# Two encoder layers in one kernel: attention scores contracted over 128 rows, norm weights spread by matmuls, and a new order at four places

## The chip, the cores and the metric

The kernel runs on one core of a Trainium2 chip, in one launch. The metric is the device time of an execution in microseconds (us); smaller is better. Engines by the names of the profile: PE (TensorE) multiplies, PEld is its loading of stationary operands, DVE (VectorE) and ACT (ScalarE) do elementwise work, POOL (GpSimd) does little here, SP (SyncE) issues the DMAs. The profile also gives the share of its full clock that TensorE was granted.

## The reference

Two layers act on x, 256 rows of 1024. Each layer is a mixer of four branches and a gated convolutional FFN; a last norm follows.

```python
for layer in range(DEPTH):                                # 2
    u = rms_norm(x, norm_mix_g[layer])
    proj = einsum('bsd,de->bse', u, w_in[layer])          # 1024 -> 8976
    (a_in, bq, bk, bv, cq, ck, cv, co, cgate, dq, dk, dv, gates) = split_cols(proj)
    y_a = fourier_mix(a_in)
    y_b = gqa_branch(bq, bk, bv, qk_norm_g[layer], cos, sin)      # 8 q heads, 2 kv heads of 64
    y_c = mlstm_branch(cq, ck, cv, co, cgate, ...)                # 4 heads of 128, both directions
    y_d = diff_branch(dq, dk, dv, ..., rel_bias, layer + 1)       # 4 heads, 2 maps of 64 each
    branch = einsum('bsnc,ncd->bsnd', stack([y_a, y_b, y_c, y_d], 2), w_branch[layer])
    merged = sum(sigmoid(gates) * branch, axis=2)
    x = x + merged @ w_out[layer]
    v = rms_norm(x, norm_ffn_g[layer])
    x = x + conv_ffn(v, w_up[layer], conv_w[layer], conv_b[layer], w_down[layer])
return rms_norm(x, final_norm_g)
```

All of it is float32. The kernel keeps near that precision by splitting an operand into a rounded part and its residual.

## The kernel before, in words

**Split operands.** `weights` (from line 158) loads a tile of weights into one of four `raw` buffers by a DMA on SP, casts it on ACT to a rounded `hi` (L167) and forms the residual `lo` on DVE (L168); `raw` is free when both are done. Their slots come from tags: `whi` and `wlo` with three each (called STD), `ys` and `L` with six and five (ALT), or single buffers borrowed from work that is over. `mm3` then runs three matmuls: hi by hi, hi by lo, lo by hi. Activations are split alike: `transposed` puts four 128x128 transposes on PE into one PSUM buffer, and `split_T` makes hi on ACT (L244, or L247 with a scale) and lo on DVE (L245, L248).

**Row tiles.** The 256 rows are two row tiles, t = 0 and 1. `normed` adds the incoming sum to x where there is one (L267), squares both halves of 512 columns on ACT (L268), finds the reciprocal root on DVE by a series of one-column operations (L201 to L206) and scales by it and by the norm's weights (L270, L273, L275, L277). `normed_T` returns a function, `place`, that puts the transposes of its result into PE's order. The norm's weights come through `gain`, a DMA that broadcasts one row of 1024 to 128 partitions (L300).

**First projections.** `first_blocks` takes, for each row tile, `place`, then k, v and mLSTM's gate columns (272 columns, L371 onwards) and then the q columns of GQA, all eight blocks of the contraction.

**The order of the work.** PE's order is the program's order: `Flow` pins each matmul and transpose behind the one before. It also runs a planned clock of PE time (matmul columns at full speed) and holds the four branches as generators; at each `tick` a branch whose wait in `LATENCY`, counted on that clock, is over puts its next step into the order. So the branches' steps lie between the weight projections. On ACT, DVE and SP the Tile scheduler orders instructions by a simulation of its own; program order sets their priority, `tc.high_priority` raises it, and `tc.issue_after(ins)` puts what a block contains behind `ins` on that engine. Slots of a tag are handed out to tiles that ask for them. ACT and DVE execute their instructions in the resulting order.

**Score calls.** In GQA's and the differential branch's `scores`, q is stacked: `stacked` writes hi of a head of 64 into one half of the 128 partitions and its residual into the other (L323, L324). The keys' hi stands in both halves, so one matmul over 128 rows yields (q_hi + q_lo) k_hi. A second matmul over 64 rows adds q_hi k_lo. One call runs eight of them; a layer has four calls in each branch. In the differential branch the two maps have stacked keys `dk[0]` and `dk[1]` (tags `L`, `bk`) and share `dk[2]` (tag `dx`), which holds each map's residual in its own half; the function `keys` fills them (L1063 to L1065).

**The out projection.** `out_proj` goes through w_out in four steps of 256 rows (`kh` 0, 2, 4, 6) by two halves of 512 columns. The first step's tiles are used for both row tiles at once. Then the second half of merged is transposed (`mT[1]`, two tiles of tag `L`; `mT[0]` has two more), then come the tiles of the other steps: STD and ALT for `kh` 2, STD for 4, and (`gate`, `mg0`), (`gate`, `mg1`) for 6. Row tile 0 is finished first, and the ffn norm runs on it while row tile 1 is multiplied.

**The FFN.** `ffn` computes the first pair of column blocks (`first_pair`) for each row tile as its norm gets ready, later pairs for all 256 rows. `up_tiles(1)`, the second pair's weights, stands behind two recorded instructions, `ends[nc.scalar]` and `ends[nc.vector]`, through `issue_after`. `down` adds the second matmul, and the next layer's norm begins as the last of it ends.

Of the kernel before, what the change touches and what calls it, by code (L numbers as in the profile page):

```python
# [10 lines left out]
F32 = mybir.dt.float32  # L11
# [8 lines left out]
P = 128  # L20
S = 256
# [9 lines left out]
NEG = -1.0e30  # L31
URGENT = 1000
MIDS = 7
LATENCY = {
    "gqa": (10.0, 3.0, 4.5, 3.2, 2.0, 1.5),
    "fourier": (2.5,),
    "mlstm": (1.7, 12.1, 3.6, 0.6, 4.6, 1.0, 2.0, 9.9, 0.8, 7.6, 5.6, 6.0, 8.0),
    "diff": (1.6, 6.0, 4.5, 2.6, 7.8),
}
EARLY = 2  # L40
# [80 lines left out]
def body(nc, tc, A, out, const, work, psum, dram):  # L121
# [119 lines left out]

    def split_T(src_ps, hi, lo, scale=None):
        if scale is None:
            nc.scalar.copy(hi, src_ps)  # L244
            nc.vector.tensor_sub(lo, src_ps, hi)  # L245
        else:
            nc.scalar.activation(hi, src_ps, AF.Copy, scale=scale)  # L247
            nc.vector.scalar_tensor_tensor(lo, src_ps, scale, hi, ALU.mult, ALU.subtract)  # L248

    def transposed(src, t, hi, lo, scale=None, at=0):  # L250
        ps = scr()
        for j in range(4):
            tr(ps[:, j * P : (j + 1) * P], src[:, j * P : (j + 1) * P], ident)
        c = slice(t * P, (t + 1) * P)
        split_T(four(ps), hi[:, at : at + 4, c], lo[:, at : at + 4, c], scale)

    ends = {}

    def normed(t, g, emit, add=None):
        with tc.high_priority(offset=URGENT):  # L260
            ss = small(2, tag="ss")
            cs = slice(0, 512), slice(512, 1024)
            xs = [x_sb[t][:, c] for c in cs]
            ys = [mid() for _ in cs]
            for half in range(2):
                if add is not None:
                    nc.vector.tensor_add(xs[half], xs[half], add[half])  # L267
                nc.scalar.activation(mid(), xs[half], AF.Square, scale=2.0 ** 13 / math.sqrt(D), accum_out=ss[:, half : half + 1])  # L268
            if add is not None:
                nc.vector.tensor_mul(ys[0], xs[0], g[:, cs[0]])  # L270
            r = rsqrt_of_two(ss)
            if add is None:
                nc.vector.scalar_tensor_tensor(ys[0], xs[0], r, g[:, cs[0]], ALU.mult, ALU.mult)  # L273
            else:
                ends[nc.scalar] = nc.scalar.activation(ys[0], ys[0], AF.Copy, scale=r)  # L275
            emit(0, ys[0])
            ends[nc.vector] = nc.vector.scalar_tensor_tensor(ys[1], xs[1], r, g[:, cs[1]], ALU.mult, ALU.mult)  # L277
            emit(1, ys[1])

    def normed_T(t, g, pair, add=None):  # L280

        halves = []
        normed(t, g, lambda half, xn: halves.append(xn), add)

        def place():
            with tc.high_priority(offset=URGENT):
                for half in range(2):
                    transposed(halves[half], t, *pair, at=4 * half)

        return place  # L290

# [6 lines left out]
    def gain(src, tag, cols, eng=None):  # L298
        g = work.tile([P, cols], F32, tag=tag, name=nm(tag))
        (eng or nc.sync).dma_start(g, src.partition_broadcast(P))  # L300
        return g

    def win(layer, c0, width):
# [59 lines left out]
    def first_blocks(uT, sets, qsets, places):  # L363
        hi, lo = uT
        kv, q = [acc() for _ in range(NT)], [acc() for _ in range(NT)]
        for t in range(NT):
# [9 lines left out]
            for k in range(KD):  # L376
                wh, wl = qsets[k // 2]
                mm3(q[t], hi[:, k, c], lo[:, k, c], wh[:, k % 2], wl[:, k % 2], k == 0, k == KD - 1)
        return kv, q

    def gqa(ps_kv, ps_q, layer, ys):
# [51 lines left out]
        for t in range(NT):  # L433
            ps = scr()
            for j in range(4):
                tr(ps[:, j * P : (j + 1) * P], qr[t][:, j * P : (j + 1) * P], ident)
            stacked(four(ps), [q2[:, :, t * P : (t + 1) * P] for q2 in qs])
        ps = scr().rearrange("p (t j c) -> p j t c", t=NT, j=2)
        for t in range(NT):
            for j in range(2):  # L440
                tr(ps[:, j, t], kr[:, t, j], ident)
        nc.scalar.copy(kh.rearrange("p j (t c) -> p j t c", t=NT), ps)
        nc.vector.tensor_sub(kl.rearrange("p j (t c) -> p j t c", t=NT), ps, kh.rearrange("p j (t c) -> p j t c", t=NT))
        yield LATENCY["gqa"][1]

        def scores(t, g):
            ps = [scr() for _ in range(2)]
            for i in range(2):
                for par in range(2):
                    rows = (top, low)[par]  # L450
# [261 lines left out]
    def diff(layer, qs, ks, v, ys):  # L712
# [16 lines left out]
        def scores(t, hp):  # L729
            ps = [scr() for _ in range(2)]  # L730
            for jh in range(2):
                for m in range(2):
                    h, rows = 2 * hp + jh, (top, low)[m]
# [90 lines left out]
    def out_proj(layer, merged, mT, g, vT):  # L824
# [10 lines left out]
        for kh in range(0, KD, 2):  # L835
            for half in range(2):
                at = ([STD, STD], [STD, ALT], [STD, STD], [("gate", "mg0"), ("gate", "mg1")])[kh // 2][half]
                late[kh, half] = tile_of(kh, half, at)
                if kh < EARLY:
                    for t in range(NT):  # L840
                        for k in (kh, kh + 1):
                            step(t, half, k, late[kh, half])
            if kh == 0:
                for t in range(NT):
                    transposed(merged[t][:, 512:], t, *mT[1], scale=0.5)
        for kh in range(EARLY, KD, 2):
            for half in range(2):
                for k in (kh, kh + 1):
# [149 lines left out]
    for layer in range(DEPTH):  # L998
        ys = {}
        if layer:  # L1000
            sets, qsets = kv_sets(layer), q_sets(layer)
        kv, q = first_blocks(uT, sets, qsets, places)
# [53 lines left out]
        flow.signal(f"co{layer}")  # L1056
        flow.tick()

        dk = [big(tag, F32R).rearrange("p (h s) -> p h s", h=4) for tag in ("L", "bk", "dx")]

        def keys(hs, ps):
            for k2, rows, others in ((dk[0], top, low), (dk[1], low, top)):
                nc.scalar.copy(k2[rows, hs], ps[rows])  # L1063
                nc.scalar.copy(k2[others, hs], ps[rows])
                nc.vector.tensor_sub(dk[2][rows, hs], ps[rows], k2[rows, hs])  # L1065

        feat_proj(uT, layer, C_DK, keys)
        ps = tok_proj(uT, win(layer, C_DV, 512))
# [99 lines left out]
```

## Time and profile before

| | us |
|---|---|
| median of 3 runs | 1072.36 |
| lowest and highest of the 3 | 1071.53, 1072.59 |
| the profiled execution | 1071.28 |
| its span | 1069.5 |
| mean granted clock of TensorE in it | 0.991 |

The profile was taken of one execution. Its span runs from the first instruction to the end of the last; 1.8 us of that execution's time lie around it. A row of a group gives line, engine, operation, out <- in with the program's names, shape and count, then busy us and mean ns of one, then the idle time ahead of it by releaser. A row of the timeline gives start, length, engine, line, operation and count, with the idle time ahead in brackets. A row of the chain gives start, length and what ran. The page's DMA lines:

```profile
q1 hardware_dynamic: 118660, 176.41, 51.0%
HBM read 175.33 MB, written 2.11 MB: 166 GB/s over the span
```

### The profile page before, as it was taken

Reading aid. Unit: us, or ns where it says so; the run is one execution under the profiler, and the core shown is the slowest. Engines: PE = TensorE matmul, PEld = TensorE weight load, DVE = VectorE, ACT = ScalarE, POOL = GpSimd, SP = SyncE. Lnnn points to the kernel's source line nnn. Section 1 sums busy time; section 2 is a strip of 40 time slices with the busy share of each in tenths; the row PEclk is TensorE's granted clock in tenths of the full one; section 3 lists DMA queues with packets and bytes.
Section 4 is the critical chain, followed back from the end, with each engine's and each line's share of the span. In section 5 each row is a group of like instructions: output and inputs, shape, how many; then the busy total and the mean of one; then the engine's idle time right before and its main releaser. Section 6 shows DMA issues by size and latency. Waiting matters only on the chain.

```text
span 1069.5 us, 15788 instructions
## 1 busy us (share of the span) xinstructions
PE 1037.3 (97%) x6024; PEld 894.5 (84%) x6024; DVE 735.9 (69%) x1380; ACT 566.7 (53%) x884; POOL 1.2 (0%) x9
## 2 busy tenths in 40 slices
PE   6999999999999999999998999999999989999997
PEld 5777997888887999999886889877888779999995
DVE  6865798787567776656678549877766677765653
ACT  4566565444445755545445656654544556654542
POOL 0000000000000000000000000000000000000000
PEclk9999999999999999999998999999999999999999
DMA  8563344545546666465334234444555556745531
GB/s 283 181 193 99 118 149 157 160 155 178 192 164 198 214 211 223 156 202 172 127 118 127 96 118 138 158 154 141 174 178 180 193 192 226 235 156 201 177 100 40
DMA packets 118735, 177.41 MB, mean 166 GB/s; under 512 B 7920, under 2 KB 69600, under 8 KB 118660
## 3 DMA queue, kind: packets, MB, share of 16 engines
q1 hardware_dynamic: 118660, 176.41, 51.0%
q8 instruction: 47, 0.77, 0.3%
q14 instruction: 28, 0.23, 0.1%
HBM read 175.33 MB, written 2.11 MB: 166 GB/s over the span
## 4 chain that ended last, share of the span: by engine, by line
PE 89%; DVE 5%; DMA 2%; ACT 2%; issue 1%; SPq 0%; ACTq 0%; DVEq 0%
PE mm L76 58%; PE at L76 29%; PE at L80 2%; DVE wlo L168 1%; DMA raw<-in_w_out_dram 1%; ACT whi L167 1%; DMA raw<-in_w_in_dram 1%; DMA raw<-in_w_up_dram 1%; DVE uT L245 0%; DVE x L267 0%; DVE rt L205 0%; ACT b L268 0%; DVE ry L206 0%; SPq L166 0%; DVE qTb L324 0%
## 5 line engine op out<-in xcount | busy, mean ns | idle before, releaser
L168 DVE TENSOR_TENSOR wlo<-raw,whi 128x1024 fp32r<-128x1024 f32 x208 | 253.4, 1223 | 117.5 <-ACT whi L167 115.4
L167 ACT CAST whi<-raw 128x1024 fp32r<-128x1024 f32 x208 | 216.9, 1048 | 181.7 <-PE mm L76 142.8
L76 PE MATMUL mm<-whi,uT 128*128 128x512 f32 x848 | 280.4, 402 | 0.0
L76 PEld LDWEIGHTS mm<-whi,uT 128*128 128x128 f32 x848 | 160.9, 190 | 38.6 <-issue 1.6
L76 PE MATMUL mm<-wlo,uT 128*128 128x512 f32 x424 | 168.2, 397 | 0.0
L167 ACT CAST ys<-raw 128x1024 fp32r<-128x1024 f32 (+1 forms) x86 | 89.7, 1044 | 44.8 <-DMA raw<-in_w_up_dram 18.6
L76 PEld LDWEIGHTS mm<-wlo,uT 128*128 128x128 f32 x424 | 80.6, 190 | 17.0
L76 PE MATMUL at<-uT,ys 128*128 128x256 f32 x480 | 88.0, 283 | 0.0
L76 PE MATMUL at<-uT,whi 128*128 128x256 f32 x480 | 86.5, 282 | 0.0
L76 PE MATMUL mm<-whi,ys 128*128 128x512 f32 x256 | 83.2, 396 | 0.0
L168 DVE TENSOR_TENSOR L<-raw,ys 128x1024 fp32r<-128x1024 f32 (+1 forms) x56 | 67.4, 1215 | 14.4 <-ACT ys L167 14.4
L76 PEld LDWEIGHTS at<-uT,ys 128*128 128x128 f32 x480 | 75.7, 191 | 1.6
L76 PEld LDWEIGHTS at<-uT,whi 128*128 128x128 f32 x480 | 74.7, 188 | 1.4
L76 PE MATMUL mm<-uT,whi 128*128 128x256 f32 x384 | 70.7, 286 | 0.0
L76 PE MATMUL at<-uT,wlo 128*128 128x256 f32 x240 | 67.6, 282 | 0.0
L76 PE MATMUL at<-uT,L 128*128 128x256 f32 x224 | 63.3, 282 | 0.0
L76 PEld LDWEIGHTS mm<-uT,whi 128*128 128x128 f32 x384 | 59.0, 189 | 1.3 <-issue 0.8
L899 DVE SCALAR_TENSOR_TENSOR b<-at,cv,b 128x255 f32<-128x255 f32 x44 | 20.9, 480 | 56.7 <-ACT b L898 56.6
L76 PEld LDWEIGHTS mm<-whi,ys 128*128 128x128 f32 x256 | 48.2, 188 | 11.3
L76 PE MATMUL mm<-ys,uT 128*128 128x256 f32 (+2 forms) x200 | 48.1, 327 | 6.5 <-DVE uT L245 3.4
L76 PE MATMUL mm<-uT,wlo 128*128 128x256 f32 x192 | 54.1, 282 | 0.0
L76 PE MATMUL mm<-ys,mg 128*128 128x512 f32 x160 | 53.7, 394 | 0.0
(280 smaller groups left out, 1831.0 us busy)
## 6 DMA issues: line engine op xcount, KB each, us to landing
raw<-in_w_in_dram SPq DMA_DIRECT2D x136, 512.0 KB
raw<-in_w_up_dram SPq DMA_DIRECT2D x88, 512.0 KB
raw<-in_w_down_dram SPq DMA_DIRECT2D x44, 512.0 KB
raw<-in_w_branch_dram SPq DMA_DIRECT2D x32, 512.0 KB
raw<-in_w_out_dram SPq DMA_DIRECT2D x16, 512.0 KB
raw<-in_w_in_dram SPq DMA_DIRECT2D x4, 384.0 KB
x<-in_x_dram SPq DMA_DIRECT2D x4, 256.0 KB
gB<-in_norm_mix_g_dram SPq DMA_DIRECT2D x2, 512.0 KB
```

The source lines that it names most:

```text
L76: self.tc.keep_in_program_order(self.nc.tensor.matmul(ps, lhsT, rhs, start=start, stop=stop))
L80: self.tc.keep_in_program_order(self.nc.tensor.transpose(ps, src, ident))
L167: nc.scalar.copy(hi[:, :n], raw[:, :n])
L168: nc.vector.tensor_sub(lo[:, :n], raw[:, :n], hi[:, :n])
L899: nc.vector.scalar_tensor_tensor(cvt[:, 1:S], a[:, 0 : S - 1], cv[:, f : f + 1], cvt[:, 1:S], ALU.mult, ALU.add)
```

## The change

It has eight parts.

1. At the start, `spread` takes the place of `gain` for the first norm's weights: two DMAs load 512 numbers each into one partition, a matmul with a stationary operand of ones (one element of the identity, broadcast) copies each to 128 partitions, and DVE moves it from PSUM to `gB`. Six matmuls on the zeroed `gpad` go ahead of everything on PE.
2. In layer 0 `first_blocks` takes keys and the first half of the q contraction for row tile 0, the same for row tile 1, and then the rest of q for both in steps of two blocks.
3. The second score matmul contracts all 128 rows with the keys' residual in both halves, in both branches. For the differential branch that takes a fourth key tile (tag `gate`) and two more subtractions in each call of `keys`.
4. GQA's splits of q and k get high priority.
5. mLSTM's second wait in `LATENCY` goes from 12.1 to 17.0; its gate columns' transposes follow that wait.
6. In `out_proj` the tiles of `kh` 2 are asked for ahead of the transposes of merged's second half, and the first step's two tiles ahead of its matmuls.
7. In `normed` with an addition, the product of the first half with the norm's weights is placed between the two halves.
8. `ends` now records the split of the transposed norm, in `place`, instead of the norm's scaling operations, so that `up_tiles(1)` stands behind that split on ACT and DVE.

```diff
+WARM = 6
-    "mlstm": (1.7, 12.1, 3.6, 0.6, 4.6, 1.0, 2.0, 9.9, 0.8, 7.6, 5.6, 6.0, 8.0),
+    "mlstm": (1.7, 17.0, 3.6, 0.6, 4.6, 1.0, 2.0, 9.9, 0.8, 7.6, 5.6, 6.0, 8.0),
...
                 nc.scalar.activation(mid(), xs[half], AF.Square, scale=2.0 ** 13 / math.sqrt(D), accum_out=ss[:, half : half + 1])
-            if add is not None:
-                nc.vector.tensor_mul(ys[0], xs[0], g[:, cs[0]])
+                if add is not None and half == 0:
+                    nc.vector.tensor_mul(ys[0], xs[0], g[:, cs[0]])
...
-                ends[nc.scalar] = nc.scalar.activation(ys[0], ys[0], AF.Copy, scale=r)
+                nc.scalar.activation(ys[0], ys[0], AF.Copy, scale=r)
             emit(0, ys[0])
-            ends[nc.vector] = nc.vector.scalar_tensor_tensor(ys[1], xs[1], r, g[:, cs[1]], ALU.mult, ALU.mult)
+            nc.vector.scalar_tensor_tensor(ys[1], xs[1], r, g[:, cs[1]], ALU.mult, ALU.mult)
...
-                    transposed(halves[half], t, *pair, at=4 * half)
+                    ends[nc.scalar], ends[nc.vector] = transposed(halves[half], t, *pair, at=4 * half)
...
+    def spread(src):
+        g = work.tile([P, D], F32, tag="gB", name=nm("gB"))
+        for half in range(2):
+            c = slice(half * 512, (half + 1) * 512)
+            row = mid()[:1]
+            nc.sync.dma_start(row, src[c].rearrange("(o d) -> o d", o=1))
+            ps = scr()
+            mm(ps, ident[0:1, 0:1].to_broadcast([1, P]), row, True, True)
+            nc.vector.tensor_copy(g[:, c], ps)
+        return g
...
+        split = KD // 2 if landing else KD
+        for t in range(NT):
+            keys(t)
+            queries(t, range(split))
+        for k in range(split, KD, 2):
+            for t in range(NT):
+                queries(t, (k, k + 1))
...
-            stacked(four(ps), [q2[:, :, t * P : (t + 1) * P] for q2 in qs])
+            with tc.high_priority(offset=URGENT):
+                stacked(four(ps), [q2[:, :, t * P : (t + 1) * P] for q2 in qs])
...
-                    mm(ps[par][:, i * S : (i + 1) * S], q2[rows], kl[rows, g], False, True)
+                    mm(ps[par][:, i * S : (i + 1) * S], q2, kl[:, g], False, True)
...
-                    mm(ps[m][:, jh * S : (jh + 1) * S], q2[rows], ks[2][rows, h], False, True)
+                    mm(ps[m][:, jh * S : (jh + 1) * S], q2, ks[2 + m][:, h], False, True)
...
+        tiles(0)
+        for half in range(2):
+            for t in range(NT):
+                for k in range(EARLY):
+                    step(t, half, k, late[0, half])
+        tiles(EARLY)
+        for t in range(NT):
+            transposed(merged[t][:, 512:], t, *mT[1], scale=0.5)
+        for kh in range(2 * EARLY, KD, 2):
+            tiles(kh)
...
+    still = gpad.rearrange("p t g c -> p (t g c)")
+    begin = acc()
+    for _ in range(WARM):
+        mm(begin[:, : 2 * P], still[:, :P], still, True, True)
     load_x(0)
-    g = gain(A["norm_mix_g"][0], "gB", D)
+    g = spread(A["norm_mix_g"][0])
...
-        dk = [big(tag, F32R).rearrange("p (h s) -> p h s", h=4) for tag in ("L", "bk", "dx")]
+        dk = [big(tag, F32R).rearrange("p (h s) -> p h s", h=4) for tag in ("L", "bk", "dx", "gate")]
...
-                nc.vector.tensor_sub(dk[2][rows, hs], ps[rows], k2[rows, hs])
+                for side in (rows, others):
+                    nc.vector.tensor_sub(l2[side, hs], ps[rows], k2[rows, hs])
```

More of the change, by code (lines that the diff above doesn't have):

```diff
@@ L243, in split_T @@
         if scale is None:
[L244 to L248, printed above, removed]
+            return nc.scalar.copy(hi, src_ps), nc.vector.tensor_sub(lo, src_ps, hi)
+        first = nc.scalar.activation(hi, src_ps, AF.Copy, scale=scale)
+        return first, nc.vector.scalar_tensor_tensor(lo, src_ps, scale, hi, ALU.mult, ALU.subtract)
     def transposed(src, t, hi, lo, scale=None, at=0):
@@ L254, in transposed @@
         c = slice(t * P, (t + 1) * P)
-        split_T(four(ps), hi[:, at : at + 4, c], lo[:, at : at + 4, c], scale)
+        return split_T(four(ps), hi[:, at : at + 4, c], lo[:, at : at + 4, c], scale)
     ends = {}
@@ L361, in q_sets, with first_blocks, keys @@
         return [weights(win(layer, C_BQ, 512)(k, 2), 2, 512, FIRST_AT[3 + k // 2]) for k in range(0, KD, 2)]
-    def first_blocks(uT, sets, qsets, places):
+    def first_blocks(uT, sets, qsets, places, landing):
         hi, lo = uT
         kv, q = [acc() for _ in range(NT)], [acc() for _ in range(NT)]
-        for t in range(NT):
+        def keys(t):
             if places[t]:
@@ L375, in first_blocks, with queries @@
             nc.vector.tensor_copy(gpad[:, t, 2:4, 0:4], gv[:, 1::2])
-            for k in range(KD):
+        def queries(t, ks):
+            c = slice(t * P, (t + 1) * P)
+            for k in ks:
                 wh, wl = qsets[k // 2]
                 mm3(q[t], hi[:, k, c], lo[:, k, c], wh[:, k % 2], wl[:, k % 2], k == 0, k == KD - 1)
+        split = KD // 2 if landing else KD
[5 more added lines that the diff above has]
+                queries(t, (k, k + 1))
         return kv, q
@@ L441, in gqa @@
                 tr(ps[:, j, t], kr[:, t, j], ident)
-        nc.scalar.copy(kh.rearrange("p j (t c) -> p j t c", t=NT), ps)
-        nc.vector.tensor_sub(kl.rearrange("p j (t c) -> p j t c", t=NT), ps, kh.rearrange("p j (t c) -> p j t c", t=NT))
+        with tc.high_priority(offset=URGENT):
+            split_T(ps, *(k.rearrange("p j (t c) -> p j t c", t=NT) for k in (kh, kl)))
         yield LATENCY["gqa"][1]
@@ L449, in scores @@
                 for par in range(2):
-                    rows = (top, low)[par]
                     q2 = qs[par][:, 2 * g + i, t * P : (t + 1) * P]
                     mm(ps[par][:, i * S : (i + 1) * S], q2, kh[:, g], True, False)
-                    mm(ps[par][:, i * S : (i + 1) * S], q2[rows], kl[rows, g], False, True)
+                    mm(ps[par][:, i * S : (i + 1) * S], q2, kl[:, g], False, True)
             pes = []
@@ L732, in scores @@
                 for m in range(2):
-                    h, rows = 2 * hp + jh, (top, low)[m]
+                    h = 2 * hp + jh
                     q2 = qs[m][:, h, t * P : (t + 1) * P]
                     mm(ps[m][:, jh * S : (jh + 1) * S], q2, ks[m][:, h], True, False)
-                    mm(ps[m][:, jh * S : (jh + 1) * S], q2[rows], ks[2][rows, h], False, True)
+                    mm(ps[m][:, jh * S : (jh + 1) * S], q2, ks[2 + m][:, h], False, True)
             b0 = (NT - 1 - t) * P
@@ L834, in out_proj, with tiles @@
         late = {}
-        for kh in range(0, KD, 2):
+        def tiles(kh):
             for half in range(2):
@@ L838, in out_proj @@
                 late[kh, half] = tile_of(kh, half, at)
[L839 to L845, printed above, removed]
+        tiles(0)
[8 more added lines that the diff above has]
+            tiles(kh)
         for kh in range(EARLY, KD, 2):
@@ L1001, in body @@
             sets, qsets = kv_sets(layer), q_sets(layer)
-        kv, q = first_blocks(uT, sets, qsets, places)
+        kv, q = first_blocks(uT, sets, qsets, places, layer == 0)
         if layer == 0:
@@ L1057, in body @@
         flow.tick()
-        dk = [big(tag, F32R).rearrange("p (h s) -> p h s", h=4) for tag in ("L", "bk", "dx")]
+        dk = [big(tag, F32R).rearrange("p (h s) -> p h s", h=4) for tag in ("L", "bk", "dx", "gate")]
         def keys(hs, ps):
-            for k2, rows, others in ((dk[0], top, low), (dk[1], low, top)):
+            for k2, l2, rows, others in ((dk[0], dk[2], top, low), (dk[1], dk[3], low, top)):
                 nc.scalar.copy(k2[rows, hs], ps[rows])
                 nc.scalar.copy(k2[others, hs], ps[rows])
-                nc.vector.tensor_sub(dk[2][rows, hs], ps[rows], k2[rows, hs])
+                for side in (rows, others):
+                    nc.vector.tensor_sub(l2[side, hs], ps[rows], k2[rows, hs])
         feat_proj(uT, layer, C_DK, keys)
```

## The prediction

> **What bounds the kernel now.** The page comes first, then TensorE's own list of waits, then the table by stretches, which also carries the granted clock.
>
> ```profile
> span 1069.5 us, 15788 instructions
> PE 1037.3 (97%) x6024; PEld 894.5 (84%) x6024; DVE 735.9 (69%) x1380; ACT 566.7 (53%) x884; POOL 1.2 (0%) x9
> ```
>
> TensorE is busy nearly all the time, so two things can be taken out: its idle 32 us, and busy time in which it runs slower than its work needs. The idle part, by releaser (columns: us, times, longest):
>
> ```profile
> PE at L80 <- DVE b L273: 8.6, 1, 8.6
> PE mm L76 <- DVE L L168: 4.5, 2, 2.2
> PE mm L76 <- DVE uT L245: 3.4, 5, 1.3
> PE mm L76 <- ACT uT L244: 3.1, 5, 1.0
> PE at L76 <- DVE mg L443: 2.8, 1, 2.8
> PE at L80 <- DVE b L574: 1.1, 1, 1.1
> PE at L80 <- ACT b L275: 0.8, 1, 0.8
> ```
>
> These are the start (8.6), a residual of w_out (twice 2.2), the transposed norms (6.5 in all) and two places of the GQA and mLSTM set-up. A wait also lowers the clock behind it:
>
> ```profile
> 36.00:56.00 20.00, 18.86 (x87) 13.97 (x85) 18.63 (x50) 12.38 (x18) 0.00 (x0) 1.00 0.66 196
> 115.00:165.00 50.00, 50.00 (x329) 45.48 (x329) 45.26 (x110) 31.72 (x49) 0.00 (x0) 1.00 0.48 153
> 310.00:330.00 20.00, 17.77 (x75) 14.15 (x74) 15.39 (x17) 10.76 (x13) 0.00 (x0) 0.91 0.57 187
> 330.00:363.00 33.00, 31.00 (x197) 27.94 (x196) 23.99 (x41) 19.50 (x29) 0.00 (x0) 0.95 0.65 211
> 560.00:590.00 30.00, 27.18 (x103) 20.34 (x102) 24.38 (x60) 18.48 (x30) 0.00 (x0) 0.83 0.41 127
> ```
>
> Columns: stretch, length, busy PE, PEld, DVE, ACT, POOL, granted clock, DMA. The clock lost is (1 - 0.91) x 20 = 1.8 us, (1 - 0.95) x 33 = 1.65 us and (1 - 0.83) x 30 = 5.1 us. VectorE is the second engine: 18.63 of 20 us in 36-56 and 45.26 of 50 in 115-165.
>
> **B, scores with 128 rows** is the largest term. Half of the score matmuls contract 64 rows, in four groups of 16 (first and last shown):
>
> ```profile
> L76 PE MATMUL at<-mg,mg 64*128 64x256 f32 x16 | 6.5, 405 | 0.0
> ...
> L76 PE MATMUL at<-dx,gq 64*128 64x256 f32 x16 | 6.1, 380 | 0.0
> ```
>
> The mean duration hides the pace, since matmuls overlap. Read starts instead: one score call is eight matmuls, alternately 128 and 64 rows. From the timeline, the first two of a call and the first instruction behind the call; from the chain, a stream of 120 matmuls of the same 256 columns, all with 128 rows:
>
> ```profile
> 591.16 0.59 PE L76 MATMUL at<-mg,qTb 128*128 128x256 f32 x2
> ```
>
> ```profile
> 593.55 0.38 PE L76 MATMUL mm<-uT,whi 128*128 128x256 f32 x1
> ```
>
> ```profile
> 363.57 14.26 PE at L76 x120
> ```
>
> A call takes 593.55 - 591.16 = 2.39 us, 0.30 per matmul; the stream runs at 14.26/120 = 0.119. With eight equal shapes and about 0.1 us for the change of tiles at the front a call would take 1.0 us, so 1.39 is saved. Two layers of four GQA and four differential calls make 16: **22 us**. The list of waits has no transpose waiting for the probabilities, and two calls and several projection steps lie between a score and its transposes, so I charge nothing for softmax having 1.4 us less. [...]
>
> Its price on VectorE: the differential keys get residuals for both halves, so four subtractions a call of `keys` instead of two.
>
> ```profile
> L1065 DVE TENSOR_TENSOR dx<-mm,bk 64x512 fp32r<-64x512 f32 x4 | 2.8, 695 | 0.1
> ```
>
> Four calls with two more each are 8 x 0.695 = 5.6 us of VectorE, 2.8 a layer, inside the stretch like 115-165 that has 4.7 us free. A projection follows before the scores need them. Bounds 0 to 5.6; I take **-1**, near the covered end. The second residual also occupies one of two `gate` slots during the first merges; the other is refilled only after a whole gate projection, so nothing there.
>
> **C, w_out's second tiles ahead of the transposes.** The tile for rows 256-511, second half, is cast long before its residual is formed:
>
> ```profile
> 313.05 1.05 ACT L167 CAST ys<-raw 128x1024 fp32r<-128x1024 f32 x1 [1.56 <-DMA raw<-in_w_out_dram]
> ```
>
> ```profile
> 324.43 1.22 DVE L168 TENSOR_TENSOR L<-raw,ys 128x1024 fp32r<-128x1024 f32 x1
> ```
>
> Ten microseconds lie between; in the code the residual's `L` slot is asked for after the two that merged's split needs. Asked for first, it can go into an earlier gap of VectorE, and TensorE's wait (2 x 2.2) goes, with layer 0's 1.8 us of clock: **6.3**. If it only moves ahead of the split's two operations (0.69 each, as the 512-column operations below), 2 x 1.25 = 2.5. The raw buffer is released earlier too, so w_up's DMAs on SP start earlier; what is late next is merged's split, which has six matmuls of `ys, L` and more in front of its reader.
>
> **D, the gates later.** In ffn the casts of the second pair stand ahead of the transposed norm's split on ScalarE:
>
> ```profile
> 349.30 1.04 ACT L167 CAST ys<-raw 128x1024 fp32r<-128x1024 f32 x1
> 350.24 1.06 ACT L244 CAST uT<-at 128x512 fp32r<-128x512 f32 x2
> ```
>
> ```profile
> 351.67 1.06 ACT L167 CAST whi<-raw 128x1024 fp32r<-128x1024 f32 x1
> ```
>
> ```profile
> 350.87 0.39 PE L76 MATMUL mm<-ys,uT 128*128 128x256 f32 x1 [0.75 <-ACT uT L244]
> ```
>
> ```profile
> 352.62 0.59 PE L76 MATMUL mm<-ys,uT 128*128 128x256 f32 x2 [1.25 <-DVE uT L245]
> ```
>
> ```profile
> 360.05 0.48 PE L76 MATMUL at<-uT,whi 128*128 128x256 f32 x2
> ```
>
> Of some 2.0 us of wait a layer (0.75 + 1.25 here) I let 0.8 stay, since a cast and a subtraction still follow the transposes; twice 1.2, and layer 0's 1.65 of clock: **4.0**. The four casts now end some 3 us later, before 360.05, when TensorE first reads them; the DMAs queued for their raw slots on SP slip as much, and that cover is what it would cost if gone, some 3 us a layer.
>
> **E and F, the norm's product between the two halves.** The product is one operation:
>
> ```profile
> L270 DVE TENSOR_TENSOR b<-x,gB 128x512 f32<-128x512 f32 x8 | 5.5, 684 | 0.0
> ```
>
> Where the halves arrive apart it leaves the path to the square root, which can end out_proj's 0.8 us wait: **+0.8**. Where both have arrived (end of layer 0, first row tile) it delays the second square: **-0.6**. The final norm is unchanged: there it runs beside the square.
>
> **A, the start.** The broadcast load of 512 KB becomes two row loads, two matmuls and two copies; six matmuls on zeros go ahead.
>
> ```profile
> 7.74 0.75 DVE L273 SCALAR_TENSOR_TENSOR b<-x,ry,gB 128x512 f32<-128x512 f32 x1 [0.72 <-DMA gB<-in_norm_mix_g_dram]
> ```
>
> ```profile
> 8.64 1.94 PE L80 MATMUL at<-ident,b 128*128 128x128 f32 x8 [8.64 <-DVE b L273]
> ```
>
> ```profile
> 25.71 10.14 PE mm L76 x53
> ```
>
> ```profile
> 264.32 44.62 PE mm L76 x192
> ```
>
> ```profile
> L227 DVE COPY b<-at 4x512 f32<-4x512 f32 x1 | 0.7, 671 | 0.0
> ```
>
> ```profile
> L76 PE MATMUL at<-b,relb 32*4 32x512 f32 x2 | 1.0, 587 | 0.0
> ```
>
> The first projections run from 8.64 to 25.71 + 10.14 = 35.85, 27.2 us. Their work at the pace of the second chain row (44.62/192 = 0.232 a 512-column matmul) is 48 x 0.232, 48 x 0.232 x 272/512 and some 2 us of transposes: 19. Of the 8 us above it, less DMA traffic ahead of the weights, t = 1's keys in place of a wait for the last q tiles, and a clock already up can save 5.5. The spread itself (two matmuls of 1.0 and two copies of 0.67) puts the gain no earlier than the load did: behind the warm-up it may be 2 us later, if the clock is low throughout. Then VectorE takes some back: stretch 36-56 has 1.4 us free, and t = 0's q now ends with t = 1's, so its reduction and three products (four operations of 512 columns like L270's, 2.7 us) come on top there. I take 2 us for that, so **3.5**; bounds -2 and 8. [...]
>
> **G, GQA's set-up first, mLSTM's columns later** (priority on q's and k's split, 12.1 to 17.0). In layer 1:
>
> ```profile
> 574.10 0.69 DVE L324 TENSOR_TENSOR qTb<-at,qTb 64x512 fp32r<-64x512 f32 x1
> ```
>
> ```profile
> 577.36 0.69 DVE L443 TENSOR_TENSOR mg<-at,mg 128x512 fp32r<-128x512 f32 x1
> 577.97 1.22 DVE L168 TENSOR_TENSOR wlo<-raw,whi 128x1024 fp32r<-128x1024 f32 x1
> ```
>
> ```profile
> 570.03 1.06 ACT L167 CAST whi<-raw 128x1024 fp32r<-128x1024 f32 x1
> ```
>
> q's residuals stand behind mLSTM's gate operations until 574.10. Moved ahead, TensorE's 2.8 us go, and 5.1 us of clock with them: 7.9 at most. But VectorE was already late: the weight cast at 570.03 gets its residual only at 577.97, after both chains, and TensorE comes to it right after the score call. Whichever chain goes first, about 3 us of that stay. I take **4.5**; bounds 0 and 7.9. Queued behind the moved splits are mLSTM's gate operations, whose transposes come 4.9 us of planned TensorE time later; mLSTM's next large step waits for `cq` anyway.
>
> **The sum** is 22 - 1 + 6.3 + 4.0 + 0.8 - 0.6 + 3.5 + 4.5 = 39.5. The profiled execution took 1071.28 (span 1069.5), so 1031.8; the median of the three, 1072.36, lies 1.1 higher, so **1033**.
>
> **The rivals.**
> 1. *Full rows do not pay.* [...] Then the calls keep 2.39 us: 1033 + 22 = 1055. Against it: the uniform streams. For it: no row of this trace has the new shapes alternating on these tiles.
> 2. *VectorE becomes the bound* where it is over 90% busy. A and G give nothing (8.0), C only 2.5 (3.8 lost), each layer's two extra key residuals stall TensorE by 1 us more (2): 13.8, so 1047. For it: 18.63 of 20 us and 45.26 of 50. Against: 69% overall, and in 115-165 TensorE waits for nothing now.
> 3. *Slower than before*: urgent splits and extra residuals push weight residuals behind TensorE's need, each time by one residual (1.22) and one fall of the clock (1.8): 3.0. There are 16 score calls and 8 calls of `keys` and q set-ups to do it: 24 x 3.0 = 72, so 1105. From 14 places on (14 x 3.0 > 39.5) the kernel is slower. Against it: the calls themselves are not moved, only their set-ups are urgent.
> 4. *Everything at its upper bound*: A 8, G 7.9, D's 1.6 left over go too: 9.5 more, 1023.
>
> **How the numbers follow.** Forecast 0.66, rival 1 0.06, rival 2 0.15, rival 3 0.03, rival 4 0.10. The range 1022 to 1046 holds the forecast with its bounds, rival 4 and about half of rival 2, some 0.83. A measurement of this kernel can tell about 0.2% from no change. Slower takes rival 3's 0.03, no change 0.01 of its milder form, faster 0.96.
>
> **What would show it.** B: score calls near 1.0 us. C: no wait of TensorE for `L` at L168, granted clock 1.00 in that stretch. D: waits for uT near 1 us a layer behind first_pair. G: no wait for `mg` at the first score call of layer 1, perhaps one for `wlo` behind it. A: first projections over at about 30 instead of 35.85, and a fuller VectorE until 50. The forecast is wrong if score calls stay above 2 us, or if new waits for `wlo` appear in the mLSTM stretches.

## The result, and the profile after

| | before | after |
|---|---|---|
| median, us (4 runs each) | 1071.94 | 1047.08 |
| lowest and highest | 1071.39, 1072.59 | 1045.55, 1049.42 |
| the profiled execution, its span | 1071.28, 1069.5 | 1045.55, 1043.4 |

The ratio is 0.977 (95% interval 0.9749 to 0.9791): 24.9 us less, where the prediction had 39.5. The time, 1047.1, lies 1 us above the range, and on the time of rival 2, though not for that rival's reasons.

From the page of after, its length and TensorE's share:

```profile
span 1043.4 us, 15823 instructions
PE 1013.9 (97%) x6040; PEld 885.1 (85%) x6040; DVE 739.2 (71%) x1390; ACT 566.0 (54%) x884; POOL 1.2 (0%) x9
```

TensorE is as full as before, in a shorter span: nearly all that went was busy time. Its list of waits in after (us, times, longest):

```profile
PE mm L77 <- DVE wlo L169: 5.4, 3, 2.4
PE at L81 <- ACT b L274: 4.1, 2, 2.1
PE at L81 <- DVE bk L452: 2.5, 1, 2.5
PE at L81 <- DVE b L272: 2.4, 1, 2.4
PE at L81 <- DVE m L584: 1.3, 1, 1.3
PE mm L77 <- ACT uT L245: 1.3, 4, 0.3
...
PE mm L77 <- DVE uT L245: 1.0, 4, 0.3
```

The waits for `L` (4.5), `uT` (6.5) and `mg` (2.8) of before are gone or small. Others stand in their place: `wlo`, `bk` and `m` are new, and the scaled half of the norm (`b` L274) has grown from 0.8.

One score call, from the timeline of after (start, length): the first of its eight matmuls, and the instruction behind it.

```profile
565.53 0.40 PE L77 MATMUL at<-mg,qTb 128*128 128x256 f32 x2
...
566.47 0.39 PE L77 MATMUL mm<-whi,uT 128*128 128x512 f32 x1
```

566.47 - 565.53 = 0.94 us, against 2.39 before. Where the rest went is seen by laying the starts of the same matmuls in both timelines side by side:

| matmul | before | after | gained by then |
|---|---|---|---|
| first of the first projections | 11.61 | 13.15 | -1.6 |
| gates' transposes, layer 0 | 36.92 | 37.37 | -0.5 |
| first score call | 55.75 | 59.85 | -4.1 |
| mLSTM's first products, layer 0 | 109.50 | 109.09 | 0.4 |
| first differential score call | 166.72 | 168.06 | -1.3 |
| merged's first transposes | 308.78 | 304.17 | 4.6 |
| conv weights' transpose, ahead of the first pair | 343.32 | 337.11 | 6.2 |
| first matmul of the second pair | 360.05 | 350.85 | 9.2 |
| first score call, layer 1 | 574.93 | 565.53 | 9.4 |
| second score call, layer 1 | 591.16 | 575.66 | 15.5 |
| merged's first transposes, layer 1 | 836.08 | 812.46 | 23.6 |
| conv weights' transpose, layer 1 | 870.09 | 845.49 | 24.6 |
| first matmul of the second pair, layer 1 | 885.26 | 859.22 | 26.0 |
| end of the last matmul | 1061.67 | 1035.58 | 26.1 |

The start loses 4.1 instead of winning 3.5; between mLSTM's products and the differential scores 1.7 a layer are lost instead of 0.5; around out_proj 2.6 are won in place of 7.1 (C and E). The first pair (4.4) and layer 1's GQA set-up (15.5 - 9.4, less the score call's own 1.4: 4.7) look as forecast. Such a table tells where time went, not which edit moved it; for G it misled.

### The profile page after: what moved, and what is told of

It is laid out like the page before. It is cut to its first block, busy times and chain, and to the rows that moved or that the text cites. A ratio compares the mean times of both kernels' runs of the same rounds, so it can differ in the third digit from the quotient of the medians.

```text
span 1043.4 us, 15823 instructions
## 1 busy us (share of the span) xinstructions
PE 1013.9 (97%) x6040; PEld 885.1 (85%) x6040; DVE 739.2 (71%) x1390; ACT 566.0 (54%) x884; POOL 1.2 (0%) x9
## 4 chain that ended last, share of the span: by engine, by line
PE 85%; DVE 6%; ACT 3%; DMA 3%; issue 2%; SPq 0%; ACTq 0%; DVEq 0%
PE mm L77 55%; PE at L77 28%; PE at L81 2%; DMA raw<-in_w_out_dram 2%; DVE wlo L169 2%; DMA raw<-in_w_up_dram 1%; ACT whi L168 1%; ACT ys L168 1%; DVE dx L1099 1%; ACT b L267 0%; DMA raw<-in_w_in_dram 0%; DVE uT L245 0%; ACT L569 0%; DVE rt L206 0%; DVE b L714 0%
## 5 line engine op out<-in xcount | busy, mean ns | idle before, releaser
L927 ACT ACTIVATE b<-at,cv 128x256 f32<-128x256 f32 x44 | 24.5, 562 | 55.0 <-PE at L77 54.6
```

The costliest lines, as they stand in the source:

```text
L927: nc.scalar.activation(cvt, a, AF.Identity, bias=cv[:, 66 + f : 67 + f], scale=cv[:, NF + f : NF + f + 1])
```

## The experiments

Eighteen kernels ran, most of them after with one edit put back or added; they are set against after's 1047.1. A median comes from four to seven runs that spread over 1 to 5 us, and the kernel before, run again beside each group of them, had medians of 1070.8 to 1072.2, so differences under some 1.5 us are not told apart.

### The start

`e1_start_old` puts back all of it, `e2_order_old` the order of the first projections, `e3_load_old` the load.

```diff
-WARM = 6
+WARM = 0                                                       # e1, e3
-    g = spread(A["norm_mix_g"][0])
+    g = gain(A["norm_mix_g"][0], "gB", D)                      # e1, e3
-        kv, q = first_blocks(uT, sets, qsets, places, layer == 0)
+        kv, q = first_blocks(uT, sets, qsets, places, False)   # e1, e2
```

> After with the whole start undone: broadcast load of the norm gain, no warm-up, first projections in the old order (t = 0 whole, then t = 1). Theory S (the start is where 7.6 us of the forecast went): the first score call comes back from 59.85 to about 55.8 us, so 1047.1 - 4.1 = 1043, or a little less if the clock behind it stays up. The prediction's own step A (the new start is worth 3.5): 1050.6. Rival V (VectorE's backlog gives a later stretch the same end whatever the start does): 1047.

> After with only the order of the first projections undone; spread and warm-up stay. Theory S, by parts: 1.55 of the loss lies ahead of the first keys matmul (the spread) and stays; the new order won 1.1 until the gates' transposes and lost 3.65 behind them (VectorE idle while both q finish together, then a reduction and products on the path to the first scores): 2.5 us faster than after, 1044.5. Rival O (the order is the good part and the spread alone is bad): 1048 or more. Rival V: 1047.

> After with the broadcast load and without the warm-up; the new order of the first projections stays. Theory S: only the 1.55 us ahead of the first keys matmul come back, 1045.5. Rival W (the warm-up's clock pays for the later start, so that without it the first projections run at half clock longer): 1047 to 1049. Look at the granted clock from 5 to 35 us and the start of the first keys matmul.

Measured: 1042.97, 1042.45 and 1046.38. Theory S has e1 right and e2 too high by 2 us: all of the loss belongs to the order, and spread and warm-up together are worth nothing that can be told from 0. VectorE's timeline of after shows the way: an idle time ahead of the first q operation, and TensorE's waits behind it.

```profile
33.17 0.69 DVE L435 TENSOR_REDUCE ssq<-b 128x8 f32<-128x512 f32 x1 [4.61 <-ACT b L434]
```

```profile
50.69 0.41 PE L81 MATMUL at<-ident,bk 128*128 128x128 f32 x2 [2.53 <-DVE bk L452]
52.43 0.44 PE L81 MATMUL at<-ident,bk 128*128 128x128 f32 x2 [1.34 <-DVE m L584]
```

Both q accumulators end together, so VectorE first has nothing (4.61 us) and then everything. (In e2 it idles 3.39 us ahead of the second q too, but has finished the first one's operations by then; its `bk` at L452 comes at 46.38 us, after's at 50.05.) `f1_q_in_turn` tests that with a third order:

```diff
-        for t in range(NT):
-            keys(t)
-            queries(t, range(split))
-        for k in range(split, KD, 2):
-            for t in range(NT):
-                queries(t, (k, k + 1))
+        keys(0)
+        queries(0, range(split))
+        keys(1)
+        queries(0, range(split, KD))
+        queries(1, range(KD))
```

> After with the first projections in a third order: keys of t = 0, half of its q, keys of t = 1, the rest of t = 0's q, then all of t = 1's q. q's last tiles still have the keys of t = 1 as cover, but the two q accumulators end 5.6 us apart (24 matmuls of 0.232) instead of 1.4. Theory Q (the loss is that both end together): the wait for bk at the transposes of layer 0 goes as with the old order, and the 1.1 us won ahead of it stay: 1041.3 to 1042.5. Rival R (having t = 1's keys early is what hurts): 1046 to 1047.

Measured: 1042.78, 0.3 above theory Q's range and well under rival R's. The first differential score call comes at 164.19 us, in e2 at 164.52 and in after at 168.06. The waits for `bk` and `m` have left TensorE's list, whose first rows are now

```profile
PE mm L77 <- DVE wlo L169: 7.9, 6, 2.4
PE at L81 <- ACT b L274: 4.0, 2, 2.1
PE at L81 <- DVE b L272: 1.9, 1, 1.9
```

The waits for `wlo` grew by 2.5 in exchange. `t = 1`'s keys early do no harm that shows; the two q's at once do. As for the warm-up, here is the pace of the first projections with it (after) and without (e3_load_old), each with the stretch from 10 to 15 us (the granted clock is the third number from the end):

```profile
15.34 0.43 PE L77 MATMUL mm<-vA,uT 128*128 128x272 f32 x1
...
16.04 0.28 PE L77 MATMUL mm<-caug,uT 128*128 128x272 f32 x1
```

```profile
10.00:15.00 5.00, 3.73 (x16) 3.33 (x17) 4.32 (x11) 3.36 (x8) 0.00 (x0) 0.50 0.95 325
```

```profile
15.48 0.43 PE L77 MATMUL mm<-vA,uT 128*128 128x272 f32 x1
...
16.35 0.29 PE L77 MATMUL mm<-hc,uT 128*128 128x272 f32 x1
```

```profile
10.00:15.00 5.00, 3.91 (x15) 3.59 (x16) 4.47 (x13) 4.80 (x10) 0.00 (x0) 1.00 0.98 336
```

Matmuls go from 0.43 to 0.29 us at about 16 us in both. In after the recorded clock is 1.00 until 8 us and 0.50 from 9 to 15 us; it falls within TensorE's wait of 2.4 us for the first norm. In e3's profile the recorded clock is 1.00 from 5 to 46 us, though its matmuls take the same 0.43 us; that they ran at half clock too is read from their pace alone. That the warm-up raised the clock neither profile shows.

### Scores of 64 rows, and the keys' residuals

`e4_rows64` puts the 64-row matmuls and the two-residual `keys` back (B undone):

```diff
-                    mm(ps[par][:, i * S : (i + 1) * S], q2, kl[:, g], False, True)
+                    mm(ps[par][:, i * S : (i + 1) * S], q2[rows], kl[rows, g], False, True)
...
-                    mm(ps[m][:, jh * S : (jh + 1) * S], q2, ks[2 + m][:, h], False, True)
+                    mm(ps[m][:, jh * S : (jh + 1) * S], q2[rows], ks[2][rows, h], False, True)
...
-                for side in (rows, others):
-                    nc.vector.tensor_sub(l2[side, hs], ps[rows], k2[rows, hs])
+                nc.vector.tensor_sub(dk[2][rows, hs], ps[rows], k2[rows, hs])
```

`e6_dk_act` leaves B and moves the second residual:

```diff
-                for side in (rows, others):
-                    nc.vector.tensor_sub(l2[side, hs], ps[rows], k2[rows, hs])
+                nc.vector.tensor_sub(l2[rows, hs], ps[rows], k2[rows, hs])
+                nc.scalar.copy(l2[others, hs], l2[rows, hs])
```

> After with the score matmuls of 64 rows and the old differential keys (two residuals a call of keys). The prediction's step B (16 calls x 1.39 = 22, each 1.4 us dearer) with the residuals' loss as read from the traces (two layers x 1.7 between the dots and the next score call): 1047.1 + 22.4 - 3.4 = 1066. With the residuals at the predicted 1 us: 1068.5. Rival H (shorter calls only expose softmax, so that part of B was never gained): under 1062.

> After with the differential keys' second residual not subtracted by VectorE from the accumulator but copied by ScalarE from the first residual, to the other 64 rows (four 64x512 operations a layer go from VectorE to ScalarE). Theory K (the extra subtractions stand ahead of the weight residuals, 1.75 us a layer): the waits for wlo between the dots and the next score call go, 1047.1 - 3.5 = 1043.6. Rival A (ScalarE waits for VectorE with weight casts queued behind, so the weights are as late as before): 1046 to 1048.

Measured: 1067.86, between e4's two sums, so B with its price is worth 20.8; and 1043.24, as theory K has it, so 3.8 of the price can be had back. Each call in e4 is some 1.5 us longer than in after, and 1.75 a layer come back between mLSTM's products and the differential scores: 16 x 1.5 - 3.5 = 20.5. The price in after, from VectorE's timeline and TensorE's:

```profile
153.83 1.38 DVE L1099 TENSOR_TENSOR dx<-mm,L 64x512 fp32r<-64x512 f32 x2
155.25 0.17 DVE L694 SCALAR_TENSOR_TENSOR den<-num 128x4 f32<-128x4 f32 x1
155.33 1.22 DVE L169 TENSOR_TENSOR wlo<-raw,whi 128x1024 fp32r<-128x1024 f32 x1
```

```profile
156.60 0.51 PE L77 MATMUL mm<-wlo,uT 128*128 128x512 f32 x1 [1.50 <-DVE wlo L169]
```

The weight residual stands behind the keys' four subtractions, and TensorE waits for it. In e6 that row is gone; of the three waits for `wlo` one is left.

### The out projection and the held tiles

`e7_out_old` puts `out_proj`'s old order back. `d1_gates_old` and `f2_out_gates_old` take the hold of the second pair's tiles away, alone and with the old order. That is more than undoing the change, since before had a hold too, behind the norm's scaling; `h1_gates_at_norm` and `h2_out_gates_at_norm` put that one back, alone and with the old order.

```diff
-                    with tc.issue_after(ends[nc.vector].ins), tc.issue_after(ends[nc.scalar].ins):
-                        tiles = up_tiles(1)
+                    tiles = up_tiles(1)                                              # d1, f2
...
-                nc.scalar.activation(ys[0], ys[0], AF.Copy, scale=r)
+                ends[nc.scalar] = nc.scalar.activation(ys[0], ys[0], AF.Copy, scale=r)   # h1, h2
...
-                    ends[nc.scalar], ends[nc.vector] = transposed(halves[half], t, *pair, at=4 * half)
+                    transposed(halves[half], t, *pair, at=4 * half)                  # h1, h2
```

> After with only out_proj's old order (second tiles behind merged's transposes). The prediction's step C as a term of its own (6.3): 1053.4. Theory N (C took the wait for the residual away, and the norm behind it, which starts earlier relative to w_up's tiles, gave most of it back as the new wait for its scaled half): the stretch from merged's transposes to the first pair won 1.6 in layer 0 and 1.0 in layer 1, so 1047.1 + 2.6 = 1049.7, with the wait for L back at about 2 us a layer and the wait for b under 1.

> After with the second pair's tiles no longer held behind the norm's split. The prediction's step D (4.0): 1051.1. Read from the traces, the first pair's stretch won 3.0 in layer 0 and 1.4 in layer 1: 1051.5. Rival (the casts are then only earlier, and the wait has another cause): 1047 to 1048.

> After with out_proj's old order and the second pair's tiles not held, both undone. If the terms were independent, the two costs add: 1047.1 + 3.2 + 10.0 = 1060.3. Theory I (with w_out's tiles early, w_up's come early too, and only the hold keeps the second pair's out of the norm's chain; in the old order they come after it anyway): the stretches of before, 7.0 dearer than after's by the traces, 1054.1, with waits like before's and the 5.2 and 5.4 us for the scaled half gone.

> After with only the hold of the second pair's tiles moved back to where it was, behind the norm's scaling operations. The prediction's step D (4.0): 1051.1. Read from the traces, the first pair's stretch won 3.0 in layer 0 and 1.4 in layer 1: 1051.5. Rival (the first pair won for another cause, the norms ready earlier for instance): 1047 to 1048.5.

> After with out_proj's old order and the hold moved back, both. If the two terms are independent: 3.2 of e7_out_old and what h1_gates_at_norm shows, 1047.1 + 3.2 + 4.4 = 1054.7. By the prediction's sizes (6.3 and 4.0): 1057.4. If the early w_up tiles are what makes the hold worth something: 1050.3 to 1052.

Measured (in the left column after, h1 and d1, in the right e7, h2 and f2):

| | new out_proj order | old order |
|---|---|---|
| hold behind the split (after's) | 1047.1 | 1050.3 |
| hold behind the scaling (before's) | 1053.1 | 1053.5 |
| no hold | 1057.1 | 1063.2 |

h1's 6.0 is more than the 4.0 to 4.4 expected; d1's 10.0 is more still, and is what no hold at all costs. The two edits together are worth 6.4; out_proj's order alone, with the old hold, 0.4 (not to be told from nothing), and the new hold alone 3.2. Theory I fell with f2, which was dearer than the two single costs, and so did the sum of independent terms with h2 (3.2 and 6.0 would be 1056.3). e7 is about what theory N had for it, 1050.3 for 1049.7: the residual's wait is back and the norm's is smaller (1.1 in all, against 4.1):

```profile
323.32 0.51 PE L77 MATMUL mm<-L,L 128*128 128x512 f32 x1 [2.23 <-DVE L L169]
...
337.69 1.09 PE L81 MATMUL at<-ident,b 128*128 128x128 f32 x8 [1.10 <-ACT b L274]
```

In after, ScalarE's timeline shows why the second grew as the first went:

```profile
326.78 1.05 ACT L168 CAST ys<-raw 128x1024 fp32r<-128x1024 f32 x1 [2.41 <-DMA raw<-in_w_up_dram]
327.74 0.62 ACT L267 ACTIVATE b<-x 128x512 f32<-128x512 f32 x1
...
328.36 1.04 ACT L168 CAST ys<-raw 128x1024 fp32r<-128x1024 f32 x1
329.30 0.62 ACT L267 ACTIVATE b<-x 128x512 f32<-128x512 f32 x1
```

```profile
334.09 1.09 PE L81 MATMUL at<-ident,b 128*128 128x128 f32 x8 [2.00 <-ACT b L274]
```

ScalarE sits 2.41 us in front of a w_up tile that DMA hasn't brought, with the square of row tile 0's first half queued behind the cast; the second square stands behind the next cast. The sums that they square were ready at 326.2 and 327.5 us. The norm now starts sooner against w_up's tiles, so they fall into its chain. `e5_held_up` moves the last two of the four tiles behind that norm's scaling:

```diff
-                nc.scalar.activation(ys[0], ys[0], AF.Copy, scale=r)
+                ends[t] = [nc.scalar.activation(ys[0], ys[0], AF.Copy, scale=r)]
             emit(0, ys[0])
-            nc.vector.scalar_tensor_tensor(ys[1], xs[1], r, g[:, cs[1]], ALU.mult, ALU.mult)
+            last = nc.vector.scalar_tensor_tensor(ys[1], xs[1], r, g[:, cs[1]], ALU.mult, ALU.mult)
+            if add is not None:
+                ends[t].append(last)
...
+                if hold and part:
+                    with tc.issue_after(ends[0][0].ins), tc.issue_after(ends[0][1].ins):
+                        res += up_part(pair, part)
...
-            tiles = up_tiles(0)
+            tiles = up_tiles(0, True)
```

> After with one thing more: the last two of the four w_up weight tiles of the first pair are cast, and their residuals formed, only behind the scaling of row tile 0's norm in out_proj. Theory N (the 2.0 and 2.1 us for which TensorE waits for ScalarE's scaled half of that norm come from these casts and residuals inside the norm's chain): both waits go, 1047.1 - 4 = 1043. Rival T (the tiles are then late for the first pair's matmuls, which read them some 3 us behind its start): the wait only moves to the w_up tiles, 1046 to 1049.

Measured: 1043.58, theory N; its list of waits has no `b` L274 any more, and `uT` for 0.4 at most.

The hold itself is read from ScalarE's timelines, first of h1 and then of after: `uT`'s cast stands behind three tiles, or ahead of them.

```profile
341.44 1.98 ACT L168 CAST whi<-raw 128x1024 fp32r<-128x1024 f32 x2
343.33 1.04 ACT L168 CAST ys<-raw 128x1024 fp32r<-128x1024 f32 x1
344.27 1.06 ACT L245 CAST uT<-at 128x512 fp32r<-128x512 f32 x2
```

```profile
343.60 1.08 ACT L245 CAST uT<-at 128x512 fp32r<-128x512 f32 x2
344.56 2.02 ACT L168 CAST whi<-raw 128x1024 fp32r<-128x1024 f32 x2
```

`f3_product_old` places the norm's product behind both halves again.

```diff
-                if add is not None and half == 0:
-                    nc.vector.tensor_mul(ys[0], xs[0], g[:, cs[0]])
+            if add is not None:
+                nc.vector.tensor_mul(ys[0], xs[0], g[:, cs[0]])
```

> After with only the norm's product back behind the second half's sum and square. The prediction's steps E and F (0.8 - 0.6): 1047.3, which can't be told from after. Rival P (the product now ahead of the second sum delays that sum and so the square, 0.7 us in the chain for which TensorE waits twice): 1045.7. Look at the two waits for the scaled half of 2.0 and 2.1 us.

Measured: 1047.42. What the product's place is worth can't be told from nothing; rival P's gain of 1.4 didn't show, and the two waits are 4.0 us in all, as in after (4.1).

### GQA's priority

`e8_gqa_old` takes the priority away, from q's splits and likewise from k's, and sets 17.0 back to 12.1, in both layers.

```diff
-    "mlstm": (1.7, 17.0, 3.6, 0.6, 4.6, 1.0, 2.0, 9.9, 0.8, 7.6, 5.6, 6.0, 8.0),
+    "mlstm": (1.7, 12.1, 3.6, 0.6, 4.6, 1.0, 2.0, 9.9, 0.8, 7.6, 5.6, 6.0, 8.0),
...
-            with tc.high_priority(offset=URGENT):
-                stacked(four(ps), [q2[:, :, t * P : (t + 1) * P] for q2 in qs])
+            stacked(four(ps), [q2[:, :, t * P : (t + 1) * P] for q2 in qs])
...
```

> After with step G undone: q's and k's splits without priority, mLSTM's columns at 12.1 again. The prediction's step G (4.5): 1051.6. Read from the traces, the stretch of layer 1 from the projections to the second score call won 6.1, of which 1.4 are the score call's own: 4.7, so 1051.8, if layer 0 adds nothing. Rival V (VectorE has the same work in either order and ends it at the same time, so the 4.7 came from something else): 1047 to 1048.

Measured: 1045.77, the 95% interval of its ratio to before 0.9744 to 0.9777, overlapping after's: step G is worth nothing that can be told, and perhaps less. e8's layer 1 has the old wait again, where after has one for `wlo` (in the order e8, after):

```profile
567.49 0.58 PE L77 MATMUL at<-mg,qTb 128*128 128x256 f32 x1 [2.81 <-DVE mg L245]
```

```profile
569.23 0.51 PE L77 MATMUL mm<-wlo,uT 128*128 128x512 f32 x1 [2.37 <-DVE wlo L169]
```

From the start of layer 1's first score call to the start of its second e8 needs 13.5 us and after 10.1, so step G wins 3.3 there (1.9 against the executions of the last section whose clock falls there). But layer 0 loses 2.2: from the gates' transposes to the fifth score call after needs 130.7 us and e8 128.5. There mLSTM's gate operations come late, and TensorE waits 1.34 us for `m`, a row that e8 hasn't. Priority and 17.0 were undone together in every run; which of them costs what was not separated.

### All together

The three causes removed at once (the edits of e2, e5 and e6), with the priority and 17.0 in both layers (c2), in none (c3, with e8's edit) and in layer 1 alone (c4); f4 is c4 with f1's order. For c4:

```diff
-        yield LATENCY["mlstm"][1]
+        yield LATENCY["mlstm"][1] if layer else 12.1
...
-            with tc.high_priority(offset=URGENT):
+            with tc.high_priority(offset=URGENT) if layer else nullcontext():
...
```

> After with the old order of the first projections, the w_up tiles held behind the norm and the differential keys' second residual on ScalarE; spread, warm-up and GQA's priority stay. If the three causes are separate places, their gains add: 1047.1 - 4.6 - 3.5 - 3.8 = 1035.2. Rival V (they are one backlog of VectorE, and the next wait takes the place of each): 1040 or more.

> The same as c2_all_g, and GQA's priority and mLSTM's 17.0 undone in both layers. Theory G (by the traces of e8_gqa_old the priority costs 2 to 3 in layer 0, where the gates' maximum then arrives late, and wins 1.3 to 2.7 in layer 1, so it is worth nothing as a whole): within 1.5 of c2_all_g. The prediction's step G (4.5 to win): c2_all_g + 4.5, 1039.7.

> The same as c2_all_g, with GQA's priority and mLSTM's 17.0 in layer 1 alone. Theory G: 1.6 to 3 less than c2_all_g and 1.3 to 2.7 less than c3_all_no_g, about 1033. If the loss in layer 0 belongs to the new order of the first projections and not to the priority: no less than c2_all_g.

> c4_all_g_second with the third order of the first projections instead of the old one. Theory Q: the old order's time less the 1.1 us that the late q tiles cost there, 1033.1 (no more than 1034.2). Rival R: 1037 or more.

Measured: 1036.68, 1036.16, 1034.24 and 1034.26. The causes are separate places: their gains add up to within 1.5 us. Step G is worth nothing in both layers together, and 2 us in layer 1 alone (theory G). The interval of c4 overlaps those of c2 and c3 a little, so this rests on the traces too: layer 1's first two score calls start 13.2 us apart in c3 and 10.2 in c4, and from layer 0's gates' transposes to its first differential score call c2 needs 125.8 us, c4 124.2. With the old order that loss of layer 0 isn't a wait for `m`: TensorE waits there for `wlo`, 2.2 us in c2 and 0.4 in c4, which has 1.2 for a tile `b` of mLSTM's gates besides. The old order serves as well as f1's, so the 1.1 us expected of that was missed. c4 beats both kernels: ratio 0.9647 (0.9634 to 0.966) to before.

## Why the prediction was wrong

| step | predicted | measured by undoing it |
|---|---|---|
| B less its residuals | 22 - 1 = 21 | 20.8 (e4) |
| C and D | 6.3 + 4.0 = 10.3 | 6.4 (h2) |
| E and F | 0.2 | 0.3 (f3) |
| A | 3.5 | -4.1 (e1) |
| G | 4.5 | -1.3 (e8) |
| sum | 39.5 | 22.1; 24.9 in all |

Three terms of the sum failed: A, which has the largest miss, then G, then the sizes of C and D. The 2.8 us between the sum and the whole are no more than the uncertainty. Undone steps needn't add (C and D don't), and each has some 1.5 us of it; taken as ratios to the kernel before that ran beside each, the five terms are 21.7, 7.1, 1.2, -3.9 and -1.0, or 25.1 in all.

**B** was right in its pace: eight equal shapes run like the 128-row stream (0.94 us a call, 1.0 forecast; rival 1 had 2.39). The 0.1 us for the change of tiles at the front was the author's estimate and does not show: 8 x 0.119 is 0.95 without it. A matmul takes 0.12 us with 128 rows throughout and 0.30 with 128 and 64 rows in turn; what makes the second slow, no run shows. That its total came out (21 and 20.8) is partly luck: the calls gave more than the sum had for them (16 x 1.5 = 24, not 22), and the residuals cost more. The term for these, "I take -1, near the covered end", was mis-sized: 3.5 to 3.8, and the cover named (a projection in between) is itself what the delayed weight residual holds up. The prediction's own sign of this, new waits for `wlo` in the mLSTM stretches, came true in both layers (1.50 us each).

**A** is the largest miss, 7.6. The failed step is "can save 5.5" less "I take 2 us for that". That six matmuls put the clock up, a part of the 5.5, was the author's estimate, and no run shows it: after, with them, records 0.50 from 9 to 15 us, and its matmuls go to 0.29 us at the time of e3's, which has none. The 5.5 weren't there: whatever the load, the warm-up and the order, the gates' transposes come between 36.6 and 37.4 us (before, after, e1, e2, e3 and f1; at 38.9 at most in any other profile). The norm's first transposes begin later, at 10.49 us for 8.64, which the prediction named ("it may be 2 us later") and left out of its sum; from there to the gates' transposes it takes 26.9 us for 28.3. The slow part of the first projections (0.43 us a matmul until 17.9 us before, 15.6 after, 15.8 in e1, whose start is that of before) was not shortened by the warm-up. What holds their end near 37 us stays open. The 2 us were twice that and more, since q's work came late as a whole: the order costs 4.6 (e2), by both q's ending together (f1).

**C** and **D**: the sizes were those of waits seen, taken as independent. D's mechanism was right, worth 6.0 with the new order (h1) and 3.2 with the old, for 4.0 forecast. C's wait went as forecast, and its gain met the wait behind it: "what is late next" had named merged's split, but it was the norm, whose chain now had w_up's tiles in it (e5 wins 3.5 by moving two of them).

**E and F** had 0.2 and measured 0.3; neither can be told from nothing, and the +0.8 and -0.6 were not taken apart. **G** had the right stretch and the right next wait (`wlo`), but its sum counted layer 1 alone, where it had 4.5 and the traces show 1.9 to 3.3. Priority and 17.0 act in layer 0 too, where no wait for `mg` could be won, and cost 2.2 there.

Of rival 2's terms, "each layer's two extra key residuals stall TensorE" held, and A and G gave nothing or less, but not because VectorE as a whole is a bound: each loss had a place of its own, and three small edits took out 10 us (c2), and keeping step G to layer 1 took out 2 more (c4). That the time fell on that rival's 1047 is chance.

## What to carry to other kernels

Give all matmuls of a run the same rows, even where a half of them multiplies a copy: here a call of eight went from 2.39 to 0.94 us. The price is in making the copy, so put that on the engine with room (in e6 that was ScalarE, and 3.8 us came back). An edit that frees TensorE somewhere must be followed to what is then late next, on every engine's queue, in each place where the same code runs. Two edits on neighbouring stretches are not two terms of a sum: undo each and both.

## What the runs showed of the hardware

Behind a wait of 2.4 us the clock fell in some executions only. The timelines of after, e1, e2, e3, e5, e6 and e7 have TensorE's wait for `wlo` in layer 1, 2.35 to 2.37 us long. In after, e2 and e7 the recorded clock stays at 1.00 behind it, and the first two score calls start 10.1 us apart. In e1, e3 and e5 it falls, to 0.63, 0.70 and 0.59 in a stretch of 4 us there, and the calls are 11.5 to 11.7 apart, as they are in e6. The stretch from 570 to 574 us, first of after (2.37 us of wait) and then of e5 (2.36):

```profile
570.00:574.00 4.00, 4.00 (x18) 2.91 (x17) 3.86 (x7) 2.36 (x5) 0.00 (x0) 1.00 0.61 171
```

```profile
570.00:574.00 4.00, 4.00 (x13) 2.59 (x11) 3.79 (x7) 2.43 (x6) 0.00 (x0) 0.59 0.66 173
```

The fall costs 1.4 to 1.5 us, which is as much as many of the steps here, and a single profile has it or hasn't. What decides between the two, no run here shows.
